# mLSTM gate logits from unsplit fp32 operands in four column groups of TensorE, with their weights loaded and folded later

## The chip, the cores and the metric

The kernel runs on one core of one Trainium2 chip. The metric is the device time of one execution in microseconds; three runs of the kernel before gave 780.39, 780.52 and 783.86, so the median is 780.52.

## The reference, cut to what matters

One encoder block on x of 512 positions by 1024 channels, batch 1, all in float32. After an RMSNorm, one projection of 10,240 columns feeds two branches: a Fourier branch (four groups of 256 channels) and an mLSTM branch (four heads of 512 channels). What the change touches is the mLSTM's gates:

```python
x_c = silu(centred_dwconv(x_m, conv_w, conv_b))      # 512 x 2048
q = block_diag_proj(x_c, w_q); k = block_diag_proj(x_c, w_k); v = block_diag_proj(x_m, w_v)   # blocks of 4
qkv = concatenate([q, k, v], axis=-1)
i_fwd = qkv @ w_igate_fwd + b_igate_fwd              # 4 heads; likewise f_fwd, i_bwd, f_bwd: 16 rows in all
```

The gate rows then go through a log-sigmoid, a cumulative sum and a running maximum, from which the heads' decay weights are made.

## The kernel before, in words

**Numbers.** A product of two fp32 matrices is made on TensorE from split operands: each tile is written once as its rounded high part (ScalarE, `hi_of`, L85) and once as the rest (VectorE, `lo_of`, L88), both in the one-pass type fp32r, and `mm3` (L93 to L97) adds high*high, high*low and low*high in PSUM. A few products (L310, L423, L618, L650 and the Fourier ones) take plain fp32 tiles instead; the trace shows each of these, the transposes of L650 apart, as two records with a weight load each.

**Weights and units.** Weights come as units of 128x1024 through `raw` (three buffers), issued on SP's queue by `fetch`; `prepare` splits them into `whi`/`wlo` (two buffers), `unit` hands the next one out. A projection unit (`proj`) is 8 x 3 = 24 products of 512 columns into one of four PSUM banks `acc`.

**The projection stage.** Seventeen units: one z unit (n = 0), then sixteen x units (n = 1 to 16) in the order `XO`. `norm_rows` (hooked in at unit 2, product group 2) makes the sums of squares, their scaling on VectorE and a power on GpSimd (L301 to L303); `norm_bcast` (hooked in by `RB_AT` at the start of unit 3) spreads the result over the partitions with four ScalarE copies, one fp32 product (L310) and a copy into `rb`. From there on `evac` (L356) takes units out of `acc`. `conv` then makes one x tile's centred convolution (one ScalarE and four VectorE instructions) and SiLU, and splits both the x tile (`vhi`, `vlo`, `so`, ...) and the convolved tile (`phi`, `plo`, ...) for the gate products.

**The gates.** `load_gates` (after unit `LOAD_AT`) brings six 256 KB pieces of gate weights over SP's queue. `fold_gates` (at `FOLD_AT`) multiplies each piece with the block-diagonal weights on GpSimd (L273), sums over four on VectorE (L274), and splits the two folded matrices into the high and low columns of `w_gate[0]` and `w_gate[1]` (L279, L280), 16 + 16 columns each. `gate_mm` (L291) then makes four products of 512 columns per tile into one bank of 32 rows: 16 tiles, 64 products. The bank is read in `gate_chain`, where a selection product (L423) adds the parts.

**Sums for later.** The last stages use sums of weight blocks that are made DRAM to DRAM. `sum_job` (called in `unit` from unit index `JOB_AT`, every third) issues a 1 MB copy on SP's queue (L156) and an accumulating one on GpSimd's (L160).

**Order.** The program order is not the order on the engines. A planner in the compiler orders each engine's instructions by their estimated ready times, earlier ones in the program first. `pin` holds an instruction behind the one traced just before it on the same engine, and nothing more. So an instruction with no inputs to wait for can move far ahead, and one that is pinned behind it can too: the load of `gb` (L414) is issued at 13.7 us though `gate_chain` comes much later in the program.

Of the kernel before, what the change touches and what calls it, by code (L numbers as in the profile page):

```python
# [8 lines left out]
F32 = mybir.dt.float32  # L9
F32R = mybir.dt.float32r  # L10
# [4 lines left out]
S = 512  # L15
D = 1024
P = 128
# [1 line left out]
EPS = 1e-6  # L19
NRAW = 3  # L20
NG = 16
JOB_AT, JOB_STEP = 8, 3
NWARM = 13
XO = (4, 5, 6, 7, 8, 9, 10, 11, 12, 13, 14, 15, 0, 1, 2, 3)
NU0 = 3
SSQ_AT, RB_AT = (2, 2), (3, 0)
LOAD_AT, FOLD_AT, CONV_AT, DRAIN_AT = 1, 4, 5, 12
Z_FIRST = 3
LOW = ("ones", "mhalf", "warm", "vecs", "raw", "whi", "wlo", "consts", "rb", "rc", "rr", "ss", "fss", "gb")
HIGH = ("sz0", "sz1", "so0", "so1", "t2k")  # L30
# [8 lines left out]
def hybrid_block(ctx: ExitStack, tc, xT, xn, units, blocks, vecs, gates, gbias, consts, dft, fnw, out):  # L39
# [37 lines left out]
    def bank(tag, cols=512, rows=P):  # L77
        count[0] += 1
        return ps.tile([rows, cols], F32, tag=tag, name=f"{tag}_{count[0]}", bufs=4)
# [4 lines left out]
    def hi_of(dst, src, scale=1.0):  # L84
        se.activation(dst, src, AF.Copy, scale=scale)  # L85
# [4 lines left out]
    def pin(ins, on=True):  # L90
        return tc.keep_in_program_order(ins) if on else ins
# [153 lines left out]
            ve.tensor_tensor(out=part[0], in0=part[0], in1=part[k], op=ALU.add)  # L245
        sqs.append(part[0])

    w_gate = [tl(f"wf{j}", [P, 16, 32], F32R) for j in range(2)]
    m4 = tl("m4", [P, 16, 4])
    prod = tl("em_r", [P, 16, 4, 4])  # L250
    ve.tensor_tensor(out=prod, in0=wkr, in1=wview(V_WQ).unsqueeze(2).to_broadcast([P, 16, 4, 4]), op=ALU.mult)
# [12 lines left out]
    def fold_gates():  # L264
        folded.append(True)
        folds = [tl("sa0", [P, 2, 16, 16]), tl("sb0", [P, 1, 16, 16])]
        for j, off in enumerate((V_WQ, V_WK, V_WV)):
            dst = folds[j // 2][:, j % 2]
            for half in range(2):
                hs = slice(8 * half, 8 * half + 8)  # L270
                g = grep[j, half]
                w = wview(off)[:, hs].unsqueeze(2).to_broadcast([P, 8, 16, 4])
                pin(gp.tensor_tensor(out=g, in0=g, in1=w, op=ALU.mult))  # L273
                ve.tensor_reduce(out=dst[:, hs, :], in_=g, axis=AX.X, op=ALU.add)  # L274
        f = folds[0]
        ve.tensor_tensor(out=f[:, 0], in0=f[:, 0], in1=f[:, 1], op=ALU.add)
        for j in range(2):
            src = folds[j][:, 0]
            se.activation(w_gate[j][:, :, 0:16], src, AF.Copy)  # L279
            ve.tensor_tensor(out=w_gate[j][:, :, 16:32], in0=src, in1=w_gate[j][:, :, 0:16].bitcast(F32), op=ALU.subtract)  # L280

    gate_ps = bank("wk", rows=32)
    pending = []
    xm, xc = {}, {}

    def gate_mm(item, last):
        p, i, ops = item
        n = 0
        for j, (h, l) in enumerate(ops):
            for r in (h, l):  # L290
                te.matmul(gate_ps, w_gate[j][:, i, :], r, start=p == 0 and n == 0, stop=last and n == 3)  # L291
                n += 1

    rb = tl("rb", [P, S])
    rc = tl("rc", [P, 4])
# [14 lines left out]
        te.matmul(rbp, ones, diag.rearrange("p b c -> p (b c)"), start=True, stop=True)  # L310
        se.activation(rb, rbp, AF.Copy)

    slots = ["plo", "so", "phi", "vhi", "vlo"]
    kept = []

    def conv(i):
        p = len(xc)
        while pending and pending[0][0] <= (p - 5 if p < 12 else p - 4):
            if not folded:
                fold_gates()  # L320
            gate_mm(pending.pop(0), False)
        src = xm[i]
        cv = t2k()
        cw = [col(V_CW + 5 * i + k) for k in range(5)]
        se.activation(cv, src, AF.Identity, scale=cw[2], bias=col(V_CB + i))
        for k, o, s in ((0, slice(2, 512), slice(0, 510)), (1, slice(1, 512), slice(0, 511)),
                        (3, slice(0, 511), slice(1, 512)), (4, slice(0, 510), slice(2, 512))):
            ve.scalar_tensor_tensor(out=cv[:, o], in0=src[:, s], scalar=cw[k], in1=cv[:, o], op0=ALU.mult, op1=ALU.add)  # L328
        if p >= 12:
            xmh, xml, xch, xcl = (tl(f"{t}{i}", [P, S], F32R) for t in ("vhi", "vlo", "phi", "plo"))  # L330
            kept.append((xch, xcl))
        elif p % 5 == 1:
            pr = [tl(f"so{n}", [P, 2, S], F32R) for n in range(2)]
            xmh, xml, xch, xcl = pr[0][:, 0, :], pr[0][:, 1, :], pr[1][:, 0, :], pr[1][:, 1, :]
        else:
            xmh, xml, xch, xcl = (tl(f"{slots[p % 5]}{n}", [P, S], F32R) for n in range(4))
        hi_of(xmh, src)
        lo_of(xml, src, xmh)
        xc[i] = tl(f"sb{i}", [P, S])
        se.activation(xc[i], cv, AF.Silu)  # L340
        hi_of(xch, xc[i])
        lo_of(xcl, xc[i], xch)
        pending.append((p, i, ((xch, xcl), (xmh, xml))))

    def proj(hooks={}):
        wh, wl = unit()
# [25 lines left out]
    for n, (kind, i) in enumerate([("z", 0)] + [("x", i) for i in XO]):  # L372
        hooks = {}
        for (at, k), fn in ((SSQ_AT, norm_rows), (RB_AT, norm_bcast)):
            if at == n:
                hooks[k] = fn
        acc = proj(hooks)
        if kind == "z":
            new_sz()
            waiting.append((None, sz[i], acc, AF.Silu))  # L380
        else:
            xm[i] = tl(f"sa{i}", [P, S])
            waiting.append((i, xm[i], acc, None))
        if n >= RB_AT[0]:
            for j, *args in waiting:
                evac(*args)
                if j is not None:
                    ready.append(j)
            waiting.clear()
        if n == LOAD_AT:  # L390
            load_gates()
        if n == FOLD_AT and not folded:
            fold_gates()
        if n >= CONV_AT and ready:
            conv(ready.pop(0))
        while n >= DRAIN_AT and ready:
            conv(ready.pop(0))
        while folded and len(pending) > (1 if n < DRAIN_AT else 2):
            gate_mm(pending.pop(0), False)
    for d in range(1, Z_FIRST):  # L400
        z_unit(d)
    while pending:
        item = pending.pop(0)
        gate_mm(item, not pending)

    a_col = tl("a_col", [P, 4, 64])
    em_r = tl("em_r", [P, S], F32R)
# [3 lines left out]
    def gate_chain():  # L411

        gb = tl("gb", [64, 2])
        nc.sync.dma_start(gb, gbias)  # L414
        graw = t2k()
        se.activation(graw[0:32, :], gate_ps, AF.Copy)
        spare = [tl(t, [64, 2, S]) for t in ("so0", "so1")]
        s0, s1, s2, s3 = spare[0][:, 0, :], spare[0][:, 1, :], spare[1][:, 0, :], spare[1][:, 1, :]
        s4, s5 = tl("wf2", [64, S]), tl("wf3", [64, S])
        ig, z, e, u, w = s0, s1, s2, s3, s4  # L420
        for j, t in enumerate((ig, z)):
            sp = bank("acc", rows=64)
            te.matmul(sp, ident_c[0:32, C_SEL + 64 * j : C_SEL + 64 * j + 64], graw[0:32, :], start=True, stop=True)  # L423
            se.activation(t[0:32, :], sp[0:32, :], AF.Identity, bias=gb[0:32, j : j + 1])
            se.activation(t[32:64, ::-1], sp[32:64, :], AF.Identity, bias=gb[32:64, j : j + 1])
        se.activation(e, z, AF.Abs)
        se.activation(e, e, AF.Exp, scale=-1.0)
        ve.tensor_scalar(out=u, in0=e, scalar1=1.0, scalar2=None, op0=ALU.add)
        ve.scalar_tensor_tensor(out=w, in0=u, scalar=-1.0, in1=e, op0=ALU.add, op1=ALU.subtract)
        se.activation(u, u, AF.Ln)  # L430
        ve.scalar_tensor_tensor(out=w, in0=z, scalar=0.0, in1=w, op0=ALU.min, op1=ALU.add)
        ve.tensor_tensor(out=w, in0=w, in1=u, op=ALU.subtract)
        fc = e
        ve.tensor_tensor_scan(out=fc, data0=ones[0:64, 0:1].to_broadcast([64, S]), data1=w, initial=0.0,
                              op0=ALU.mult, op1=ALU.add)
# [12 lines left out]
        return an  # L448
# [527 lines left out]
def _layouts(inputs):  # L976
# [63 lines left out]
    for dr in range(2):  # L1040
        for h in range(4):
            consts[32 * dr + h, C_BSEL + 4 * dr + h] = 1.0
            consts[64 + 32 * dr + h, C_BSEL + 4 * dr + h] = 1.0
            for j in range(2):
                for part in range(2):
                    consts[16 * part + 8 * j + 4 * dr + h, C_SEL + 64 * j + 32 * dr + h] = 1.0
    sc = 1.0 / np.sqrt(512.0 * 256.0)
    c = np.arange(256)[:, None]
    k = np.arange(129)[None, :]
# [30 lines left out]
```

## Time and profile before

| | |
|---|---|
| Median of three runs | 780.52 us (780.39 to 783.86) |
| The profiled execution | 782.93 us, its span 781.0 us |
| TensorE (PE) busy | 766.3 us, 98% of the span |
| VectorE (DVE), ScalarE (ACT), GpSimd (POOL) busy | 525.0, 417.4, 67.2 us |
| Mean granted TensorE clock | 0.995 of full speed |

Times in rows are microseconds from the span's start unless a column says ns. A matmul's record lasts longer than the place it takes, since the next one starts while it drains; what a product costs in a gapless stretch is the distance between starts. "busy" of an instruction that is held up by another engine includes the hold. In the waits and in brackets after a row, the name behind `<-` is what ended the idle time.

### The profile page before, as it was taken

Reading aid. Unit: us, or ns where it says so; the run is one execution under the profiler, and the core shown is the slowest. Engines: PE = TensorE matmul, PEld = TensorE weight load, DVE = VectorE, ACT = ScalarE, POOL = GpSimd, SP = SyncE. Lnnn points to the kernel's source line nnn. Section 1 sums busy time; section 2 is a strip of 40 time slices with the busy share of each in tenths; the row PEclk is TensorE's granted clock in tenths of the full one; section 3 lists DMA queues with packets and bytes.
Section 4 is the critical chain, followed back from the end, with each engine's and each line's share of the span. In section 5 each row is a group of like instructions: output and inputs, shape, how many; then the busy total and the mean of one; then the engine's idle time right before and its main releaser. Section 6 shows DMA issues by size and latency. Waiting matters only on the chain.

```text
span 781.0 us, 10974 instructions
## 1 busy us (share of the span) xinstructions
PE 766.3 (98%) x4182; PEld 654.9 (84%) x4182; DVE 525.0 (67%) x802; ACT 417.4 (53%) x658; POOL 67.2 (9%) x139
## 2 busy tenths in 40 slices
PE   9799999999999999999999999999999999999996
PEld 7587777778888888888888888899999999988885
DVE  6799998577857664777485972156676787446632
ACT  7356556568646743685363542266544587534422
POOL 0400000010210210021101000000011100000021
PEclk9999999999999999999999999999999999999999
DMA  8747762054363545155604582366555356445511
GB/s 300 235 141 209 214 179 92 28 161 138 80 189 102 167 109 162 42 174 154 197 27 162 141 257 90 105 193 217 190 161 159 121 166 192 144 144 169 172 55 55
DMA packets 39446, 117.03 MB, mean 150 GB/s; under 512 B 4577, under 2 KB 5090, under 8 KB 35298
## 3 DMA queue, kind: packets, MB, share of 16 engines
q1 hardware_dynamic: 37090, 99.56, 37.8%
q0 software_dynamic: 2304, 16.78, 11.2%
q8 instruction: 33, 0.54, 0.3%
q14 instruction: 19, 0.16, 0.1%
HBM read 114.22 MB, written 35.65 MB: 192 GB/s over the span
## 4 chain that ended last, share of the span: by engine, by line
PE 93%; DVE 2%; DMA 2%; ACT 2%; issue 0%; SPq 0%; POOL 0%; POOLq 0%; ACTq 0%; DVEq 0%
PE acc L95 16%; PE acc L97 16%; PE acc L96 16%; PE wk L95 7%; PE wk L97 7%; PE wk L96 7%; PE acc L548 3%; PE acc L547 3%; PE acc L549 3%; PE wk L291 2%; PE acc L955 2%; PE acc L953 2%; PE acc L954 2%; PE wk L618 2%; DMA raw<-in_units_dram 2%; DVE wlo L88 1%
## 5 line engine op out<-in xcount | busy, mean ns | idle before, releaser
L88 DVE TENSOR_TENSOR wlo<-raw,whi 128x1024 fp32r<-128x1024 f32 (+1 forms) x103 | 128.4, 1249 | 84.0 <-ACT whi L85 83.9
L85 ACT ACTIVATE whi<-raw 128x1024 fp32r<-128x1024 f32 (+1 forms) x103 | 106.4, 1034 | 135.2 <-PE acc L96 98.0
L97 PE MATMUL acc<-hhi,wlo 128*128 128x512 f32 x248 | 97.3, 393 | 4.3 <-DVE wlo L88 4.3
L95 PE MATMUL acc<-hhi,whi 128*128 128x512 f32 x248 | 97.8, 397 | 0.8 <-ACT whi L85 0.8
L96 PE MATMUL acc<-hlo,whi 128*128 128x512 f32 x248 | 97.7, 394 | 0.0
L97 PEld LDWEIGHTS acc<-hhi,wlo 128*128 128x128 f32 x248 | 47.0, 190 | 15.5 <-DVE wlo L88 4.7
L95 PEld LDWEIGHTS acc<-hhi,whi 128*128 128x128 f32 x248 | 46.8, 189 | 11.6 <-ACT whi L85 1.2
L96 PEld LDWEIGHTS acc<-hlo,whi 128*128 128x128 f32 x248 | 47.0, 190 | 11.3 <-DVE hlo L199 0.7
L549 PE MATMUL acc<-whi,hlo 128*128 128x512 f32 x128 | 50.4, 394 | 0.0
L548 PE MATMUL acc<-wlo,hhi 128*128 128x512 f32 x128 | 50.4, 393 | 0.0
L96 PE MATMUL acc<-sb,whi 128*128 128x512 f32 x128 | 49.9, 391 | 0.0
L95 PE MATMUL acc<-sa,whi 128*128 128x512 f32 x128 | 49.8, 390 | 0.1
L96 PE MATMUL wk<-vlo,phi 128*128 128x512 f32 x128 | 49.8, 389 | 0.0
L95 PE MATMUL wk<-vhi,phi 128*128 128x512 f32 x128 | 49.8, 390 | 0.0
L97 PE MATMUL acc<-sa,wlo 128*128 128x512 f32 x128 | 48.6, 391 | 0.0
L97 PE MATMUL wk<-vhi,plo 128*128 128x512 f32 x128 | 48.0, 389 | 0.0
L547 PE MATMUL acc<-whi,hhi 128*128 128x512 f32 x128 | 47.7, 393 | 0.0
L328 DVE SCALAR_TENSOR_TENSOR t2k<-sa,vecs,t2k 128x511 f32<-128x511 f32 (+1 forms) x64 | 45.6, 739 | 0.0
L88 DVE TENSOR_TENSOR gwl<-raw,gwh 128x1024 fp32r<-128x1024 f32 x27 | 33.0, 1222 | 15.9 <-ACT gwh L85 15.9
L85 ACT ACTIVATE gwh<-raw 128x1024 fp32r<-128x1024 f32 x27 | 28.6, 1059 | 18.3 <-PE acc L96 8.3
L95 PEld LDWEIGHTS wk<-vhi,phi 128*128 128x128 f32 x128 | 24.0, 188 | 5.8 <-issue 0.8
L95 PEld LDWEIGHTS acc<-sa,whi 128*128 128x128 f32 x128 | 24.0, 188 | 5.4 <-ACT whi L85 0.5
(352 smaller groups left out, 1956.9 us busy)
## 6 DMA issues: line engine op xcount, KB each, us to landing
raw<-in_units_dram SPq DMA_DIRECT2D x77, 512.0 KB, 3.4
sum<-in_blocks_dram SPq DMA_DIRECT2D x16, 1024.0 KB, 6.5
raw<-sum SPq DMA_DIRECT2D x64, 256.0 KB, 3.8
raw<-in_blocks_dram SPq DMA_DIRECT2D x48, 256.0 KB, 3.7
sum<-in_blocks_dram POOLq DMA_DIRECT2D x8, 1024.0 KB, 8.2
sum<-sum POOLq DMA_DIRECT2D x8, 1024.0 KB, 8.8
xr<-in_xT_dram SPq DMA_DIRECT2D x8, 256.0 KB, 4.2
yb<-in_xn_dram SPq DMA_DIRECT2D x8, 256.0 KB, 2.6
```

Source lines behind the costliest of these rows:

```text
L85: se.activation(dst, src, AF.Copy, scale=scale)
L88: ve.tensor_tensor(out=dst, in0=src, in1=hi.bitcast(F32), op=ALU.subtract)
L95: pin(te.matmul(acc, wh, xh, start=start, stop=False, **skip), pinned)
L96: te.matmul(acc, wh, xl, start=False, stop=False, **skip)
L97: te.matmul(acc, wl, xh, start=False, stop=stop, **skip)
L291: te.matmul(gate_ps, w_gate[j][:, i, :], r, start=p == 0 and n == 0, stop=last and n == 3)
L328: ve.scalar_tensor_tensor(out=cv[:, o], in0=src[:, s], scalar=cw[k], in1=cv[:, o], op0=ALU.mult, op1=ALU.add)
L547: te.matmul(ops[t], hv(x_hi, k)[:, ts], wh[:, ks], start=k == 0, stop=False)
L548: te.matmul(ops[t], hv(x_hi, k)[:, ts], wl[:, ks], start=False, stop=False)
L549: te.matmul(ops[t], hv(x_lo, k)[:, ts], wh[:, ks], start=False, stop=k == 7)
L618: te.matmul(vp[:, ds], xm[c0 + d][:, b * P : (b + 1) * P], vbf[:, d, :], start=True, stop=True)
L953: te.matmul(acc, m_hi[k][:, ts], wh, start=k == 0, stop=False)
```

## The change

- The x tiles and convolved tiles are no longer split for the gates; only the last four convolved tiles still are (they are used by the first head).
- `gate_mm` takes the fp32 tiles themselves. It runs on four tiles (two pairs) at a time, once more than four are pending. Each of the eight products has 32 weight columns (16 used, 16 zero) and goes to one of four groups of 32 columns of the array, and so to one of four groups of 32 rows of a 128-row bank: convolved and x tile, of the first and of the second of a pair. 32 fp32 products replace 64 of type fp32r.
- `w_gate` is plain fp32, zeroed at the start on GpSimd; the split of the folded weights goes.
- The six multiplications of the fold move from GpSimd to VectorE.
- Gate weights are loaded after unit 6 instead of 1, and folded at unit 10 instead of 4; `conv` begins at unit 4 instead of 5.
- `norm_bcast` is hooked in at product group 6 of unit 2 instead of at the start of unit 3.
- `JOB_AT` goes from 8 to 11.
- The selection product adds four row groups instead of two.

```diff
-JOB_AT, JOB_STEP = 8, 3
+JOB_AT, JOB_STEP = 11, 3
-SSQ_AT, RB_AT = (2, 2), (3, 0)
-LOAD_AT, FOLD_AT, CONV_AT, DRAIN_AT = 1, 4, 5, 12
+SSQ_AT, RB_AT = (2, 2), (2, 6)
+LOAD_AT, FOLD_AT, CONV_AT, DRAIN_AT = 6, 10, 4, 12
...
-    w_gate = [tl(f"wf{j}", [P, 16, 32], F32R) for j in range(2)]
+    w_gate = [tl(f"wf{j}", [P, 16, 32]) for j in range(2)]
+    for j in range(2):
+        gp.memset(w_gate[j], 0.0)
...
-                pin(gp.tensor_tensor(out=g, in0=g, in1=w, op=ALU.mult))
+                ve.tensor_tensor(out=g, in0=g, in1=w, op=ALU.mult)
                 ve.tensor_reduce(out=dst[:, hs, :], in_=g, axis=AX.X, op=ALU.add)
         f = folds[0]
-        ve.tensor_tensor(out=f[:, 0], in0=f[:, 0], in1=f[:, 1], op=ALU.add)
-        for j in range(2):
-            src = folds[j][:, 0]
-            se.activation(w_gate[j][:, :, 0:16], src, AF.Copy)
-            ve.tensor_tensor(out=w_gate[j][:, :, 16:32], in0=src, in1=w_gate[j][:, :, 0:16].bitcast(F32), op=ALU.subtract)
-
-    gate_ps = bank("wk", rows=32)
+        ve.tensor_tensor(out=w_gate[0][:, :, 0:16], in0=f[:, 0], in1=f[:, 1], op=ALU.add)
+        se.activation(w_gate[1][:, :, 0:16], folds[1][:, 0], AF.Copy)
+    gate_ps = bank("wk")
...
-    def gate_mm(item, last):
-        p, i, ops = item
-        n = 0
-        for j, (h, l) in enumerate(ops):
-            for r in (h, l):
-                te.matmul(gate_ps, w_gate[j][:, i, :], r, start=p == 0 and n == 0, stop=last and n == 3)
-                n += 1
+    def gate_mm(items):
+        for a in range(0, len(items), 2):
+            for b in range(2):
+                p, i = items[a + b]
+                for j, r in enumerate((xc[i], xm[i])):
+                    rows = slice(32 * (2 * b + j), 32 * (2 * b + j) + 32)
+                    te.matmul(gate_ps[rows, :], w_gate[j][:, i, :], r, start=p < 2, stop=p >= 14,
+                              tile_position=(0, 32 * (2 * b + j)))
...
-        if p >= 12:
-            xmh, xml, xch, xcl = (tl(f"{t}{i}", [P, S], F32R) for t in ("vhi", "vlo", "phi", "plo"))
-            kept.append((xch, xcl))
-        elif p % 5 == 1:
...
-        hi_of(xmh, src)
-        lo_of(xml, src, xmh)
         xc[i] = tl(f"sb{i}", [P, S])
         se.activation(xc[i], cv, AF.Silu)
-        hi_of(xch, xc[i])
-        lo_of(xcl, xc[i], xch)
-        pending.append((p, i, ((xch, xcl), (xmh, xml))))
+        if p >= 12:
+            xch, xcl = (tl(f"{t}{i}", [P, S], F32R) for t in ("phi", "plo"))
+            hi_of(xch, xc[i])
+            lo_of(xcl, xc[i], xch)
+            kept.append((xch, xcl))
+        pending.append((p, i))
...
-        while folded and len(pending) > (1 if n < DRAIN_AT else 2):
-            gate_mm(pending.pop(0), False)
+        if folded and len(pending) >= 5:
+            gate_mm([pending.pop(0) for _ in range(4)])
     for d in range(1, Z_FIRST):
         z_unit(d)
-    while pending:
-        item = pending.pop(0)
-        gate_mm(item, not pending)
+    gate_mm(pending)
```

## Rows read from the trace of the kernel before

**Rows 1.** The page's busy time of each engine, and the busy time by stretch (us of the stretch, then PE, PEld, DVE, ACT, POOL busy with instruction counts, granted clock, DMA share, GB/s).

```profile
PE 766.3 (98%) x4182; PEld 654.9 (84%) x4182; DVE 525.0 (67%) x802; ACT 417.4 (53%) x658; POOL 67.2 (9%) x139
...
0.00:33.00 33.00, 26.12 (x119) 20.97 (x120) 21.48 (x26) 18.40 (x33) 8.96 (x17) 1.00 0.88 285
33.00:140.00 107.00, 107.00 (x462) 82.62 (x462) 100.55 (x147) 63.80 (x95) 4.21 (x5) 0.98 0.57 167
...
30.00:40.00 10.00, 7.24 (x25) 5.83 (x26) 10.00 (x13) 3.64 (x6) 1.61 (x2) 0.83 0.44 130
```

**Rows 2.** What PE waited for in the first 200 us (us in total, times, longest).

```profile
PE acc L97 <- DVE wlo L88: 4.3, 1, 4.3
PE wk L181 <- POOL half L457: 1.1, 1, 1.1
PE acc L95 <- ACT whi L85: 0.8, 1, 0.8
PE wk L310 <- ACT sa L308: 0.7, 1, 0.7
```

**Rows 3.** The timeline of VectorE, GpSimd, ScalarE and SP's queue around 24 us (start, duration, engine, line, what).

```profile
13.71 0.55 SPq L414 DMA_DIRECT2D gb<-in_gbias_dram  x1
14.94 0.54 SPq L156 DMA_DIRECT2D sum<-in_blocks_dram  x1
15.57 1.01 SPq L126 DMA_DIRECT2D raw<-in_units_dram  x2
...
22.01 0.16 DVE L302 TENSOR_SCALAR rc<-wk 128x4 f32<-128x4 f32 x1 [2.05 <-PE wk L301]
23.25 1.08 POOL L160 DMA_DIRECT2D sum<-in_blocks_dram  x1 [21.99 <-DMA sum<-in_blocks_dram]
24.17 1.36 POOL L303 TENSOR_TENSOR rc<-rc,mhalf 128x4 f32<-128x4 f32 x1
24.27 1.06 ACT L85 ACTIVATE whi<-raw 128x1024 fp32r<-128x1024 f32 x1 [6.25 <-DMA raw<-in_units_dram]
25.20 3.39 POOL L273 TENSOR_TENSOR sa<-sa,vecs 128x512 f32<-128x512 f32 x3
25.36 7.35 DVE L88 TENSOR_TENSOR wlo<-raw,whi 128x1024 fp32r<-128x1024 f32 x1 [3.19 <-ACT whi L85]
25.56 1.28 ACT L308 ACTIVATE sa<-consts,rc 128x128 f32<-128x128 f32 x4 [0.23 <-POOL rc L303]
28.26 3.35 POOL L273 TENSOR_TENSOR sb<-sb,vecs 128x512 f32<-128x512 f32 x3
33.82 1.21 DVE L88 TENSOR_TENSOR wlo<-raw,whi 128x1024 fp32r<-128x1024 f32 x1
```

**Rows 4.** PE's timeline from the last sums of squares (L301) to the return of the full clock; from 21.84 to 25.78 it has 18 products without a gap.

```profile
21.61 0.36 PE L301 MATMUL wk<-ones,sb 128*128 128x1 f32 x2
21.84 0.48 PE L95 MATMUL acc<-hhi,so 128*128 128x512 f32 x1
...
25.78 0.39 PE L97 MATMUL acc<-hhi,so 128*128 128x512 f32 x1
26.89 1.13 PE L310 MATMUL wk<-sa,ones 128*128 128x512 f32 x2 [0.72 <-ACT sa L308]
...
28.09 0.39 PE L96 MATMUL acc<-hlo,whi 128*128 128x512 f32 x1
32.76 0.58 PE L97 MATMUL acc<-hhi,wlo 128*128 128x512 f32 x1 [4.29 <-DVE wlo L88]
33.13 0.63 PE L95 MATMUL acc<-hhi,whi 128*128 128x512 f32 x1
...
36.51 0.39 PE L97 MATMUL acc<-hhi,wlo 128*128 128x512 f32 x1
36.74 0.40 PE L95 MATMUL acc<-hhi,whi 128*128 128x512 f32 x1
```

**Rows 5.** The gate products: one of the groups by tile (durations min/median/max in ns, weights 128*32), and two pieces of the chain of waits (start, length, what).

```profile
L291 PE MATMUL wk<-plo,wf x16: 387/392/398, 56.3 to 137.8; 128*32 128x512 f32 x16
...
81.58 0.93 PE wk L291 x4
...
98.71 0.93 PE wk L291 x4
```

**Rows 6.** The plain fp32 products in the chain of waits: L423 (32 rows, 64 weight columns, 512 moving columns) and L618 (128x128, 128 moving columns), each record one of two per product; and L618's form by line (busy us, mean ns).

```profile
140.91 1.86 PE acc L423 x4
...
170.87 1.56 PE wk L618 x14
...
178.85 1.78 PE wk L618 x16
...
L618 PE MATMUL wk<-mhi,sa 128*128 128x128 f32 x128 | 16.7, 274 | 0.0
```

**Rows 7.** The timeline around L423 (PE products and PEld weight loads).

```profile
140.53 0.39 PE L95 MATMUL wk<-vhi,phi 128*128 128x512 f32 x1
140.84 0.19 PEld L423 LDWEIGHTS acc<-t2k,consts 32*64 32x64 f32 x2 [0.35 <-issue]
140.85 1.93 PE L423 MATMUL acc<-t2k,consts 32*64 32x512 f32 x4
...
142.70 0.19 PEld L95 LDWEIGHTS wk<-vhi,phi 128*128 128x128 f32 x1 [0.81 <-issue]
142.70 0.50 PE L95 MATMUL wk<-vhi,phi 128*128 128x512 f32 x1
...
143.04 0.39 PE L96 MATMUL wk<-vlo,phi 128*128 128x512 f32 x1
```

**Rows 8.** VectorE and ScalarE instructions by form between 33 and 140 us (busy us, mean ns, idle before): the weight split, one of the gate splits on each engine, the fold's sums, and a VectorE product with a broadcast operand.

```profile
L88 DVE TENSOR_TENSOR wlo<-raw,whi 128x1024 fp32r<-128x1024 f32 x17 | 20.7, 1215 | 0.7 <-ACT whi L85 0.7
L88 DVE TENSOR_TENSOR plo<-sb,phi 128x512 fp32r<-128x512 f32 x4 | 2.7, 680 | 0.0
L274 DVE TENSOR_REDUCE sa<-sa 128x128 f32<-128x512 f32 x3 | 1.9, 672 | 0.0
L471 DVE TENSOR_TENSOR t2k<-m,consts 128x512 f32<-128x512 f32 x1 | 0.7, 682 | 0.0
...
L85 ACT ACTIVATE phi<-sb 128x512 fp32r<-128x512 f32 x6 | 3.8, 628 | 0.1
```

More of the change, by code (lines that the diff above doesn't have):

```diff
@@ L311, in norm_bcast @@
         se.activation(rb, rbp, AF.Copy)
-    slots = ["plo", "so", "phi", "vhi", "vlo"]
     kept = []
@@ L317, in conv @@
         p = len(xc)
-        while pending and pending[0][0] <= (p - 5 if p < 12 else p - 4):
-            if not folded:
-                fold_gates()
-            gate_mm(pending.pop(0), False)
         src = xm[i]
@@ L328, in conv @@
             ve.scalar_tensor_tensor(out=cv[:, o], in0=src[:, s], scalar=cw[k], in1=cv[:, o], op0=ALU.mult, op1=ALU.add)
-        if p >= 12:
-            xmh, xml, xch, xcl = (tl(f"{t}{i}", [P, S], F32R) for t in ("vhi", "vlo", "phi", "plo"))
-            kept.append((xch, xcl))
-        elif p % 5 == 1:
[L333 to L336, printed above, removed]
-        hi_of(xmh, src)
-        lo_of(xml, src, xmh)
         xc[i] = tl(f"sb{i}", [P, S])
         se.activation(xc[i], cv, AF.Silu)
-        hi_of(xch, xc[i])
-        lo_of(xcl, xc[i], xch)
-        pending.append((p, i, ((xch, xcl), (xmh, xml))))
+        if p >= 12:
[4 more added lines that the diff above has]
+        pending.append((p, i))
     def proj(hooks={}):
@@ L397, in hybrid_block @@
             conv(ready.pop(0))
-        while folded and len(pending) > (1 if n < DRAIN_AT else 2):
-            gate_mm(pending.pop(0), False)
+        if folded and len(pending) >= 5:
+            gate_mm([pending.pop(0) for _ in range(4)])
     for d in range(1, Z_FIRST):
         z_unit(d)
-    while pending:
-        item = pending.pop(0)
-        gate_mm(item, not pending)
+    gate_mm(pending)
     a_col = tl("a_col", [P, 4, 64])
@@ L415, in gate_chain @@
         graw = t2k()
-        se.activation(graw[0:32, :], gate_ps, AF.Copy)
+        se.activation(graw, gate_ps, AF.Copy)
         spare = [tl(t, [64, 2, S]) for t in ("so0", "so1")]
@@ L422, in gate_chain @@
             sp = bank("acc", rows=64)
-            te.matmul(sp, ident_c[0:32, C_SEL + 64 * j : C_SEL + 64 * j + 64], graw[0:32, :], start=True, stop=True)
+            te.matmul(sp, ident_c[:, C_SEL + 64 * j : C_SEL + 64 * j + 64], graw, start=True, stop=True)
             se.activation(t[0:32, :], sp[0:32, :], AF.Identity, bias=gb[0:32, j : j + 1])
@@ L1044, in _layouts @@
             for j in range(2):
-                for part in range(2):
-                    consts[16 * part + 8 * j + 4 * dr + h, C_SEL + 64 * j + 32 * dr + h] = 1.0
+                for part in range(4):
+                    consts[32 * part + 8 * j + 4 * dr + h, C_SEL + 64 * j + 32 * dr + h] = 1.0
     sc = 1.0 / np.sqrt(512.0 * 256.0)
```

## The prediction, made before the changed kernel ran

> **What bounds the kernel now.** I read the busy time first, whole and by stretch. TensorE works for 766 of 781 us, and from 33 to 140 us, where the gates are made, it never pauses: 107.0 of 107.0 us [rows 1]. VectorE is next, busy for 100.6 of those 107 us. So in that stretch only what changes TensorE's own work changes the time; VectorE's load counts only if it grows. The first 33 us are different: PE works for 26.1 us of them, and the list of its waits has one large entry, 4.3 us for one weight split [rows 2]. The timelines show its cause: the split starts at 25.36 and takes 7.35 us, where the next of its kind takes 1.21 [rows 3]. It ends when GpSimd's six multiplications of the fold (25.20 to 31.6) are over: for that time VectorE got nothing done that PE needed. Then the clock: the ten microseconds from 30 have a mean granted clock of 0.83 [rows 1], and after the pause the products start 0.43 us apart instead of 0.227 until 36.5 [rows 4], the lower of the two levels, 1.2 instead of 2.4 GHz.
>
> **The start of the kernel.** Three terms, in starts of PE instructions [rows 4].
>
> (a) The pause goes, since no multiplication is left on GpSimd. The product at 28.09 should have been followed at 28.32; the next one started at 32.76: 4.4 us. What is late next in its place? Unit 3's weights landed at 24.27 behind 1.5 MB of gate weights and a 1 MB block copy; the gate weights now come after unit 6, so unit 3 comes no later. Its two splits take 1.06 and 1.21 us [rows 3], and PE reaches unit 3 at about 27 us: no wait follows.
>
> (b) Without the pause the clock stays up. From 32.76 to 36.51 nine products took 3.75 us instead of 9 x 0.227 = 2.04: 1.7 us. The other two runs of the kernel before are some 2.5 us shorter than the profiled one, so they may have lost less here; I take 1.7, with 0 as the low end.
>
> (c) `norm_bcast` moves from the end of unit 2 to 12 products after the sums of squares, 21.84 + 12 x 0.227 = 24.6. Its chain is the scaling (ends 22.17), GpSimd's power (1.36), four copies (1.28) and hand-overs. Before, the power stood behind a block-sum DMA on GpSimd until 24.17 [rows 3]. That one is a job traced after the `gb` load: the copy at 14.94 is pinned to it and so floats to the front. With `JOB_AT` 11 a job falls on the same place in the program (20 - 8 and 20 - 11 are both multiples of 3), so a 1 MB copy still floats; but it is then job 3, and the accumulating DMA after it needs results of jobs 1 and 2, so it can't stand ahead of the power. The chain then ends at about 22.2 + 0.1 + 1.36 + 1.28 + 0.1 = 25.0, and PE waits 0.4 us for it. Before, the product started at 26.89 where 26.0 was possible, 0.9 us. Gain 0.5; from 0 (GpSimd held as before) to 0.9.
>
> Together 4.4 + 1.7 + 0.5 = 6.6 us, between 4.4 and 7.0.
>
> **The gate products.** Before: four in 0.93 us, so 64 x 0.2325 = 14.9 us of gapless PE time [rows 5]. After: 32 fp32 products, which are 64 records, each of two passes. A record of 512 columns isn't there in a full-speed stretch; its price is bounded by L423, 1.86 / 4 = 0.465, and by L618, 1.56 / 14 = 0.111 for 128 columns, four times that 0.446 [rows 6]. I take 0.445; narrow weights (L423) load late, which groups of eight would hide. One after another, that is 28.5 us. What the column groups give back no row shows: every product of this kernel writes from row 0 and has the whole array to itself. Neighbouring products of the change use different groups, but the two records of one product use the same one. If records start in the order of issue, the second record of a product waits for the first and holds up all behind it; then it runs beside the first record of the next product. A run of n products takes n + 1 record times. With four runs of eight: 36 x 0.445 = 16.0 us. To this comes the change of mode: around L423 the products start 0.32 and 0.34 us apart where 0.227 is usual, 0.1 us at each end [rows 7], 0.2 per run, 0.8 for four. So 16.8 us, 1.9 more than before. The ends: all four groups at once, 16 x 0.445 + 0.8 = 7.9 (7.0 less than before); none, 28.5 + 0.8 = 29.3 (14.4 more). I take the middle since it is what issue in order gives; if the planner puts other products between, each further run costs 0.445 + 0.2.
>
> The Trainium skill's page "TensorE: Matmul & The Clock Gate" (Part 3: Packing small matmuls) has matmuls of different tiles overlap while they start and end strictly in the order of issue, which is the middle case. Its page "TensorEngine Tiling (Array Packing)" (Key Properties) says that a change of tiling mode drains the engine; the 0.1 us at each end of L423 would be that.
>
> **What lies beside other work.** 28 gate splits go on each of two engines: 28 x 0.68 = 19.0 us on VectorE, 28 x 0.63 = 17.6 on ScalarE [rows 8]. PE never waited for either from 33 to 140 us, so this gives nothing. The six multiplications add 6 x 0.68 = 4.1 us to VectorE, which has 16 us net more room by then; I cost them at nothing (rival D has the case without room). The zeroing of `w_gate` is two writes on GpSimd, idle from 1.3 to 23 us. The six gate loads now stand on SP's queue behind unit 9's weights, with unit 10's behind them. SP's issues take up to about half a microsecond, so these come some 3 us later, while two units of 5.4 us each are split or ready ahead: nothing; at most the 3 us. The block sums are first used after unit 63 and the last job moves by one step, to unit index 59; on GpSimd every later job stands where one stood before: nothing. An earlier `conv` fills VectorE while it idles.
>
> **Sum.** The profiled execution took 782.9 us for a span of 781.0. 782.9 - 6.6 + 1.9 = 778.2; against the median, which is 2.4 lower, 780.5 - 6.6 + 1.9 = 775.8: 776.
>
> **The rivals.**
>
> A, slower: the column groups don't overlap; the gate block is 14.4 us longer, and 780.5 - 6.6 + 14.4 = 788.3. The kernel becomes slower once 64 records take more than 14.9 + 6.6 - 0.8 = 20.7 us, 47 record times. For it: no row shows two products in the array at once, and both records of L423, with a quarter of the array's rows, had it to themselves. Against it: the groups share no cell and no output row.
>
> C: four records run side by side, because a record that waits for its group doesn't hold up the others: 780.5 - 6.6 - 7.0 = 766.9. For it: neighbours are four different groups. Against it: it needs a record to overtake the one ahead, and in the timeline every product starts in the order of its weight load. "TensorEngine Tiling (Array Packing)" in the Trainium skill (Key Properties) says that tiles operate independently, with weight loads and matmuls in parallel; taken at its word that is C, and no row here decides.
>
> D: the fold on VectorE becomes PE's wait. Six multiplications, six sums and an addition, close to 0.6 us apart, are 7.5 us. A weight split may start when the unit two before it is done, so it has 5.4 + 0.5 - 1.1 - 1.2 = 3.6 us to spare; a fold in one piece ahead of it stops PE for 3.9: 775.8 + 3.9 = 779.7. For it: VectorE is 94% busy there today. Against: the planner puts ready instructions in gaps, as it did with the sums of the fold, and the load falls by 16 us.
>
> E, the change doesn't do what it says: something else holds the split of unit 3, and the pause stays. Then 780.5 + 1.9 = 782.4. Against it: the pause's only cause in the rows is on GpSimd.
>
> **How the numbers follow.** Forecast 0.38, C 0.29, A 0.17, D 0.11, E 0.05. Half a per cent, 3.9 us, is about what a measurement of this kernel can tell from no change: faster is below 776.6, slower above 784.4. Faster: all of C, 0.23 of the forecast's 0.38 (it lies 0.8 from that bound and one run more costs 0.65), 0.01 of D: 0.53. Same: 0.15 of the forecast, 0.10 of D, 0.05 of E: 0.30. Slower: A, 0.17. The range from 764.5 to 783.5 takes in all but A. The likeliest case alone reaches from 775 (terms b and c at their best) to 779 (b at half, three runs more).
>
> **What would show it.** (a) No entry of PE waiting for `wlo` in the first 40 us, and no split near 7 us. (b) Granted clock 1.00 from 30 to 40 us. (c) L310 starts near 25.0. Gates: records of 32 weight columns start in pairs, a pair every 0.445 us; single ones every 0.445 us show A, four to 0.445 us show C. D: a wait of PE for `wlo` near 70 us with L273's successors just before it on VectorE. The prediction is wrong if the gate records together hold PE for much less or more than 17 us, or if a new wait stands in the first 33 us.

## The result, and the profile after

Fifteen runs of the changed kernel have a median of 776.04 us (775.46 to 776.96), fifteen of the kernel before 780.52 (775.57 to 783.86): a ratio of 0.9947, 95% interval 0.9927 to 0.9967. The forecast was 776.0. The profiled execution took 776.38 us.

The page's span and busy times of the changed kernel answer to [rows 1]:

```profile
span 774.7 us, 10917 instructions
...
PE 763.4 (99%) x4182; PEld 647.3 (84%) x4182; DVE 507.0 (65%) x778; ACT 401.0 (52%) x629; POOL 61.7 (8%) x135
```

Its busy time in the same three stretches as in [rows 1], with the same columns:

```profile
0.00:33.00 33.00, 30.99 (x142) 24.89 (x143) 17.45 (x29) 19.96 (x35) 2.54 (x12) 1.00 0.70 237
33.00:140.00 107.00, 105.61 (x462) 75.05 (x461) 87.05 (x120) 50.87 (x71) 4.61 (x5) 1.00 0.56 163
30.00:40.00 10.00, 10.00 (x43) 7.71 (x42) 8.29 (x13) 5.43 (x7) 0.00 (x0) 1.00 0.17 53
```

PE is busy 4.9 us longer in the first 33 us, and at full clock from 30 to 40 us. From 33 to 140 us it had no pause before; now 1.39 us are missing. The list of what PE waited for from 9 to 200 us says where:

```profile
PE acc L95 <- ACT whi L85: 1.4, 2, 0.9
PE wk L577 <- ACT vhi L85: 0.5, 1, 0.5
```

The entry of 4.3 us for `wlo` [rows 2] is gone, and a pair for `whi` is new. (Line numbers have moved: the broadcast L310 is now L311, `evac` L345, the fold L275 and L276, the gate products L292.)

A ledger over the projection stage needs marks. I take the starts of the 96th and the 480th projection product (L95 to L97), the last of the fourth and of the twentieth unit of 24. The timeline of the kernel before has them here:

```profile
39.27 0.39 PE L97 MATMUL acc<-hhi,wlo 128*128 128x512 f32 x1
...
157.35 0.39 PE L97 MATMUL acc<-hhi,wlo 128*128 128x512 f32 x1
```

The changed kernel's timeline around the start:

```profile
22.78 1.02 POOL L304 TENSOR_TENSOR rc<-rc,mhalf 128x4 f32<-128x4 f32 x1 [20.60 <-DVE rc L303]
...
29.94 1.02 PE L311 MATMUL wk<-sa,ones 128*128 128x512 f32 x2
...
31.71 0.69 DVE L345 TENSOR_TENSOR sz<-acc,rb 128x512 f32<-128x512 f32 x1 [7.50 <-ACT rb L312]
...
32.19 0.39 PE L97 MATMUL acc<-hhi,wlo 128*128 128x512 f32 x1
...
151.05 0.39 PE L97 MATMUL acc<-hhi,wlo 128*128 128x512 f32 x1
```

So the start gains 39.27 - 32.19 = 7.1 us, and the later mark, like the span, 6.3. The gates add 1.4 to the 7.1, and 2.2 go back.

**The gates.** Their timeline, the longest run of records and a short one:

```profile
67.46 0.39 PE L97 MATMUL acc<-hhi,wlo 128*128 128x512 f32 x1
67.78 0.62 PE L292 MATMUL wk<-sb,wf 128*32 128x512 f32 x1
67.78 0.62 PE L292 MATMUL wk<-sa,wf 128*32 128x512 f32 x1
67.79 0.62 PE L292 MATMUL wk<-sb,wf 128*32 128x512 f32 x1
67.80 0.62 PE L292 MATMUL wk<-sa,wf 128*32 128x512 f32 x1
68.23 0.59 PE L292 MATMUL wk<-sb,wf 128*32 128x512 f32 x1
...
69.63 0.50 PE L97 MATMUL acc<-hhi,wlo 128*128 128x512 f32 x1
69.97 0.40 PE L95 MATMUL acc<-hhi,whi 128*128 128x512 f32 x1
...
121.15 1.04 PE L292 MATMUL wk<-sb,wf 128*32 128x512 f32 x2
122.13 0.50 PE L95 MATMUL acc<-hhi,whi 128*128 128x512 f32 x1
```

Four records start within 0.02 us, and the next four 0.43 us later: all four groups work side by side. As the cost of a run I take the time from the last product ahead of it to the second behind it, less 2 x 0.227. The long run of 16 records (eight products) costs 69.97 - 67.46 - 0.45 = 2.06; runs of 4 to 6 records cost 1.2, and so does the single product at 121.15. The planner made ten runs, 13.6 us in all; the kernel before spent 15.0 by the same measure, in 26 runs.

**What goes back.** From 32.19 the next 144 products, all ahead of the first gate run, take 34.81 us; at the 5.44 us that a unit of 24 takes in a gapless stretch they would take 32.64. That is the 2.2 us. Most of it stands at the two new waits. The changed kernel's timeline at the first of them:

```profile
53.45 1.22 DVE L88 TENSOR_TENSOR wlo<-raw,whi 128x1024 fp32r<-128x1024 f32 x1
54.32 1.06 ACT L85 ACTIVATE whi<-raw 128x1024 fp32r<-128x1024 f32 x1 [1.07 <-PE acc L96]
54.35 0.39 PE L95 MATMUL acc<-hhi,whi 128*128 128x512 f32 x1
54.58 0.39 PE L96 MATMUL acc<-hlo,whi 128*128 128x512 f32 x1
55.44 0.50 PE L95 MATMUL acc<-hhi,whi 128*128 128x512 f32 x1 [0.47 <-ACT whi L85]
55.77 0.40 PE L96 MATMUL acc<-hlo,whi 128*128 128x512 f32 x1
56.01 0.40 PE L97 MATMUL acc<-hhi,wlo 128*128 128x512 f32 x1
```

The usual order is L95, L96, L97. Here L95 and L96 come twice before the L97. The program's order on TensorE, with the tiles numbered, tells why (`acc_112` is the next unit):

```
L95 MATMUL acc_105_548<-hhi0_14_122,whi_95_501 128x512 [waits Activation_49]
L96 MATMUL acc_105_548<-hlo0_18_126,whi_95_501 128x512
L95 MATMUL acc_112_589<-hhi0_14_122,whi_102_542 128x512 [waits Activation_49]
L96 MATMUL acc_112_589<-hlo0_18_126,whi_102_542 128x512
L97 MATMUL acc_105_548<-hhi0_14_122,wlo_96_502 128x512 [waits DVE_49]
```

The planner put two products of the next unit ahead of the product that needs the low part. But the next unit's split has to wait for one of the two `whi` buffers, until the unit before is done (54.32), and PE stands until it is finished. The low part that the planner was avoiding was ready at 53.45 + 1.22 = 54.67, before the 54.81 at which its product could have started. The same order stands one unit on (a wait of 0.92 us until 62.11). With the slow restarts (54.58 to 55.44 and 60.80 to 62.11 where 0.23 is usual, then 0.1 each) the two cost 1.9 of the 2.2 us.

The medians differ by 4.5, not 6.3 to 6.5: the profiled run of the kernel before lies 2.4 above its median.

### The profile page after: what moved, and what is told of

Its sections match the earlier page's. It is cut to its first block, busy times and chain, and to the rows that moved or that the text cites. A ratio compares the mean times of both kernels' runs of the same rounds, so it can differ in the third digit from the quotient of the medians.

```text
span 774.7 us, 10917 instructions
## 1 busy us (share of the span) xinstructions
PE 763.4 (99%) x4182; PEld 647.3 (84%) x4182; DVE 507.0 (65%) x778; ACT 401.0 (52%) x629; POOL 61.7 (8%) x135
## 4 chain that ended last, share of the span: by engine, by line
PE 96%; ACT 1%; DVE 1%; DMA 1%; SPq 0%; issue 0%; POOL 0%; POOLq 0%; ACTq 0%
PE acc L95 17%; PE acc L97 17%; PE acc L96 17%; PE wk L97 7%; PE wk L95 7%; PE wk L96 7%; PE acc L534 3%; PE acc L535 3%; PE acc L536 3%; PE acc L942 2%; PE acc L941 2%; PE acc L940 2%; PE wk L605 2%; PE wk L292 1%; PE wk L637 1%; DMA raw<-in_units_dram 1%
## 5 line engine op out<-in xcount | busy, mean ns | idle before, releaser
L88 DVE TENSOR_TENSOR wlo<-raw,whi 128x1024 fp32r<-128x1024 f32 (+1 forms) x103 | 122.3, 1190 | 80.6 <-ACT whi L85 80.3
L95 PE MATMUL acc<-hhi,whi 128*128 128x512 f32 x248 | 97.2, 395 | 1.7 <-ACT whi L85 1.7
L97 PE MATMUL acc<-hhi,wlo 128*128 128x512 f32 x248 | 97.2, 393 | 0.0
L96 PE MATMUL acc<-hlo,whi 128*128 128x512 f32 x248 | 97.0, 391 | 0.0
L95 PEld LDWEIGHTS acc<-hhi,whi 128*128 128x128 f32 x248 | 46.5, 188 | 15.0 <-ACT whi L85 4.6
L97 PEld LDWEIGHTS acc<-hhi,wlo 128*128 128x128 f32 x248 | 46.6, 188 | 14.7 <-DVE sa L345 2.5
L96 PEld LDWEIGHTS acc<-hlo,whi 128*128 128x128 f32 x248 | 46.6, 188 | 10.0 <-DVE hlo L199 0.7
L96 PE MATMUL acc<-sb,whi 128*128 128x512 f32 x128 | 49.9, 391 | 0.0
L95 PE MATMUL acc<-sa,whi 128*128 128x512 f32 x128 | 49.8, 390 | 0.1
L96 PE MATMUL wk<-vlo,phi 128*128 128x512 f32 x128 | 49.8, 389 | 0.0
L95 PE MATMUL wk<-vhi,phi 128*128 128x512 f32 x128 | 49.6, 390 | 0.0
L97 PE MATMUL acc<-sa,wlo 128*128 128x512 f32 x128 | 48.6, 391 | 0.0
L97 PE MATMUL wk<-vhi,plo 128*128 128x512 f32 x128 | 48.0, 389 | 0.0
L95 PEld LDWEIGHTS wk<-vhi,phi 128*128 128x128 f32 x128 | 24.0, 188 | 5.7 <-PE acc L410 0.8
L95 PEld LDWEIGHTS acc<-sa,whi 128*128 128x128 f32 x128 | 24.0, 188 | 5.4 <-ACT whi L85 0.5
```

The lines of the kernel that those rows point to most:

```text
L88: ve.tensor_tensor(out=dst, in0=src, in1=hi.bitcast(F32), op=ALU.subtract)
L95: pin(te.matmul(acc, wh, xh, start=start, stop=False, **skip), pinned)
L96: te.matmul(acc, wh, xl, start=False, stop=False, **skip)
L97: te.matmul(acc, wl, xh, start=False, stop=stop, **skip)
```

## The experiments

Twelve runs. A median stands with its ratio to the kernel before, timed on the same chip; one profiled execution each gives the marks. The changed kernel was timed with the result alone, so a difference from it sets two medians of different timings side by side; its own fifteen runs lie within 1.5 us.

**1. The kernel before, with only the fold's multiplications on VectorE.**

```diff
-                pin(gp.tensor_tensor(out=g, in0=g, in1=w, op=ALU.mult))
+                ve.tensor_tensor(out=g, in0=g, in1=w, op=ALU.mult)
```

> The kernel before with one edit: the six multiplications of the fold on VectorE instead of GpSimd. Theory 1 (the 7.35 us weight split and PE's 4.3 us pause come from GpSimd's multiplications): no weight split over 1.5 us after 20 us, no wait of PE for it in the first 40 us, full clock from 30 to 40 us; about 4.4 + 1.7 us less, 774 to 777. Rival (unit 3 is late because its transfer is late): the pause stays, 779 to 782.

Median 779.78, ratio 0.9992 (0.9964 to 1.0019): the cause of the pause was right, the time a miss. The 4.3 us pause is gone, but the unpinned multiplications now stand on VectorE ahead of work that PE needs. Timeline:

```profile
20.12 1.28 DVE L273 TENSOR_TENSOR sa<-sa,vecs 128x512 f32<-128x512 f32 x2
20.25 0.50 PE L96 MATMUL acc<-hlo,whi 128*128 128x512 f32 x1 [0.52 <-DVE hlo L199]
...
22.05 0.38 PE L301 MATMUL wk<-ones,sb 128*128 128x1 f32 x2 [0.60 <-DVE sb L245]
```

and the stretches behind it:

```profile
20.00:25.00 5.00, 4.15 (x20) 3.53 (x21) 3.22 (x7) 2.12 (x2) 1.07 (x1) 0.80 1.03 372
25.00:30.00 5.00, 5.00 (x14) 3.90 (x13) 4.42 (x7) 1.28 (x4) 1.96 (x1) 0.52 1.02 236
```

After the two short pauses the clock is at its lower level until 29.8, with 14 products in 5 us where 22 fit. The 96th product starts at 37.16: only 2.1 us gained. Taking the multiplications off GpSimd is not enough.

**2. The changed kernel, with the multiplications back on GpSimd** (the line of run 1, the other way).

> The changed kernel with one edit undone: the six multiplications back on GpSimd, pinned as before. Theory 1: wherever they run, a VectorE instruction with two operands in SBUF is held up for some 6.7 us in all; VectorE is full there and a weight split has about 3.6 us to spare, so PE waits some 3 us: 778 to 780. Rival (only the place at 25 us made it costly): 775 to 777, or less, since VectorE is relieved of 4.1 us.

778.68, ratio 0.9996 (0.9966 to 1.0027): 2.6 slower than the changed kernel, as expected. Timeline:

```profile
46.94 4.32 POOL L275 TENSOR_TENSOR sa<-sa,vecs 128x512 f32<-128x512 f32 x3 [23.51 <-ACT sb L326]
51.22 4.53 POOL L275 TENSOR_TENSOR sb<-sb,vecs 128x512 f32<-128x512 f32 x3
...
63.09 0.79 PE L97 MATMUL acc<-hhi,wlo 128*128 128x512 f32 x1 [2.48 <-DVE wlo L88]
```

The start keeps its gain (96th product at 32.21), so the late place alone clears it, wherever the multiplications run. A pause for `wlo` comes back behind the fold's new place, with a granted clock of 0.78 from 60 to 65 us, in place of the pair for `whi`; the gates cost 14.4.

**3. All gate products in one column group** (a bank of 32 rows, same sums).

```diff
-    gate_ps = bank("wk")
+    gate_ps = bank("wk", rows=32)
...
-                    te.matmul(gate_ps[rows, :], w_gate[j][:, i, :], r, start=p < 2, stop=p >= 14,
-                              tile_position=(0, 32 * (2 * b + j)))
+                    te.matmul(gate_ps, w_gate[j][:, i, :], r, start=p + j == 0, stop=p + j == 16,
+                              tile_position=(0, 0))
```

> The changed kernel with all 32 gate products in one column group and one group of 32 rows of the bank; the same sums, made one after another. Theory 2 (the column groups let products run at once): 64 records at 0.43 us are 27.5 us plus about 0.34 us for each run of them, so 14 to 18 us more than the changed kernel, 790 to 794. Rival (narrow fp32 products overlap anyway, or PE's time isn't set by them): 776 to 779.

792.83, ratio 1.017 (1.012 to 1.022), 16.8 above the changed kernel; the gates take 30.1 us. Timeline:

```profile
67.65 1.04 PE L291 MATMUL wk<-sb,wf 128*32 128x512 f32 x2
68.54 1.02 PE L291 MATMUL wk<-sa,wf 128*32 128x512 f32 x2
69.39 1.02 PE L291 MATMUL wk<-sb,wf 128*32 128x512 f32 x2
```

Products 0.857 us apart, two records of 0.428 each: what rival A would have been.

**4. Gates at the end of the program, unpinned.**

```diff
-        if folded and len(pending) >= 5:
-            gate_mm([pending.pop(0) for _ in range(4)])
```

> The changed kernel with all 32 gate products in one go after the last projection unit. Theory 2: a run costs two records' time (0.86 us) for every four products begun plus 0.34 us, so one run of 32 products takes 7.2 us instead of the 13.6 us of the ten runs in the changed kernel: 6.4 us less, about 770. Rival (the gate chain then starts later and the first head waits for it): most of that comes back as a wait of PE between 140 and 175 us, 773 to 778.

775.35, ratio 0.9927 (0.99 to 0.9953): a miss. The planner floated the products forward again, in nine runs, 12.4 us.

**5. The same, each gate product pinned.**

```diff
-                    te.matmul(gate_ps[rows, :], w_gate[j][:, i, :], r, start=p < 2, stop=p >= 14,
-                              tile_position=(0, 32 * (2 * b + j)))
+                    pin(te.matmul(gate_ps[rows, :], w_gate[j][:, i, :], r, start=p < 2, stop=p >= 14,
+                                  tile_position=(0, 32 * (2 * b + j))))
```

> The changed kernel with all 32 gate products after the last projection unit and each pinned behind the one before, so that they stay one run. Theory 2 (four products at a time, 0.34 us for each run of them): 16 record times of 0.428 us plus 0.34 us is 7.2 us, where the ten runs of the changed kernel take 13.6; 6.4 us less, 769 to 771. Rival (the runs stood where PE would have waited for weight splits or the gate chain, so packing them uncovers those waits): new waits of PE between 60 and 175 us, 773 to 777.

769.54, ratio 0.988 (0.9826 to 0.9934). One run of 64 records; the chain of waits has it as

```profile
115.76 7.00 PE wk L292 x64
```

7.2 us with its ends, 6.4 less than in ten runs; the time fell by 6.5. The price of a run follows: 64 records in fours are 16 starts, 16 x 0.428 (run 3) = 6.85, and 0.35 remains for the run itself.

**6. As 5, with the two products of each column group next to each other in the order of issue.**

```diff
-        for a in range(0, len(items), 2):
-            for b in range(2):
-                p, i = items[a + b]
-                for j, r in enumerate((xc[i], xm[i])):
+        for a in range(0, len(items), 4):
+            for b in range(2):
+                for j in range(2):
+                    for c in range(2):
+                        p, i = items[a + 2 * c + b]
+                        r = (xc, xm)[j][i]
```

> As a_end_pinned, but in each block of eight products the two of one column group stand next to each other. Theory 3 (products start in the order of issue, and one whose group is busy holds up those behind it): each pair of neighbours of one group costs two record times, 34 in all, 14.6 us plus 0.34, about 7.7 us more than a_end_pinned. Rival (a product of a free group overtakes): 7 to 8 us for the run, as in a_end_pinned.

770.48 in a single run; the gates take 7.28 us. Instructions are issued sb, sb, sa, sa; the timeline shows

```profile
116.57 0.62 PE L294 MATMUL wk<-sb,wf 128*32 128x512 f32 x1
116.58 0.62 PE L294 MATMUL wk<-sa,wf 128*32 128x512 f32 x1
116.59 0.62 PE L294 MATMUL wk<-sb,wf 128*32 128x512 f32 x1
116.61 0.62 PE L294 MATMUL wk<-sa,wf 128*32 128x512 f32 x1
```

A start of every group within 0.04 us: a product whose group is free does not wait behind one whose group is busy. Starts strictly in order fall.

**7. The changed kernel, with the gate weights loaded and folded early.**

```diff
-LOAD_AT, FOLD_AT, CONV_AT, DRAIN_AT = 6, 10, 4, 12
+LOAD_AT, FOLD_AT, CONV_AT, DRAIN_AT = 1, 4, 4, 12
```

> The changed kernel with the gate weights loaded after unit 1 and folded at unit 4 as before, the multiplications still on VectorE. Theory 4 (it takes the late load as well: early multiplications stand ahead of the last splits of x on VectorE, PE pauses shortly and its clock falls): pauses of about 0.5 us near 20 us, a granted clock well below 1 between 20 and 30 us, 3 to 4 us more than the changed kernel, 779 to 780. Rival (moving the multiplications was enough): 775 to 777.

781.34, ratio 1.003 (0.9998 to 1.0062): the whole gain is gone. The pauses of run 1 are back (0.52 at 20.07, 0.61 at 21.88), but in the profiled execution, 779.69, the clock stayed up:

```profile
20.00:25.00 5.00, 4.32 (x25) 3.54 (x26) 3.51 (x8) 1.65 (x2) 0.00 (x0) 1.00 1.01 344
25.00:30.00 5.00, 5.00 (x24) 4.12 (x23) 5.00 (x9) 1.75 (x5) 1.93 (x1) 1.00 0.66 219
```

So there the start costs only 1.6 us (96th product at 33.79), and the rest has another reason than the one given: the gates, ready earlier, come in 14 runs instead of 10, 17.4 us, 3.8 more. The pair of waits for `whi` is absent, 2.2 less; together 3.2 of the 3.3 us between the two profiled executions. The other 2 us of the median are not in this profile: the three executions above 782.7 us have a mean granted clock of 0.993, the two below 780 have 0.997 and 0.999.

**8. The changed kernel, with the hook of `norm_bcast` and `JOB_AT` as before.**

```diff
-JOB_AT, JOB_STEP = 11, 3
+JOB_AT, JOB_STEP = 8, 3
-SSQ_AT, RB_AT = (2, 2), (2, 6)
+SSQ_AT, RB_AT = (2, 2), (3, 0)
```

> The changed kernel with two edits undone: the norm's broadcast at the start of unit 3 and the block sums from unit index 8. As the prediction has it: the accumulating DMA stands ahead of the power on GpSimd again, and the broadcast is 1 to 2 us later; PE loses about 0.5 us, 776 to 777. Rival (these two edits carry a large part of the 7.1 us gained by unit 4): 778 to 780, with a wait of PE before 40 us.

773.75, ratio 0.9921 (0.9892 to 0.995): 2.3 better than the changed kernel, a miss of mine. Timeline:

```profile
19.37 1.07 POOL L160 DMA_DIRECT2D sum<-in_blocks_dram  x1 [17.19 <-DMA sum<-in_blocks_dram]
...
26.23 1.02 PE L311 MATMUL wk<-sa,ones 128*128 128x512 f32 x2
...
27.92 0.69 DVE L345 TENSOR_TENSOR sz<-acc,rb 128x512 f32<-128x512 f32 x1 [3.82 <-ACT rb L312]
```

With the earlier hook the broadcast runs later: 29.94 against 26.23. VectorE then stood idle for 7.5 us where it is 3.8 here. With the old hook the pair of waits for `whi` is gone, the program's order on TensorE has no product of the next unit ahead of an L97, and the gates come in eight runs, 12.9 us.

**9 and 10. As 5, with the old hook; and with the old `JOB_AT` too** (lines of run 8).

> a_end_pinned with the norm's broadcast at the start of unit 3 again, the block sums still from index 11. Theory 5 (the hook in unit 2 made the planner put the broadcast behind unit 3, so that VectorE idled 7.5 us and PE waited 1.4 us later): broadcast near 26 us, no waits of PE at 55 and 62 us, 1.4 to 2.3 us less than a_end_pinned, 767 to 768. Rival (the gain of a_rb_job_old came from the block sums): 769 to 770.

> As a_end_pinned_rb_old, and the block sums from index 8 again. Theory 5: the block sums' place changes nothing, so the same as a_end_pinned_rb_old within 0.5 us, 767 to 768. Rival (they matter): 1 us or more apart from it.

768.08 (767.51 to 769.05), ratio 0.9849 (0.9793 to 0.9906), and 768.22, ratio 0.985 (0.9793 to 0.9906). Both beat both kernels; the place of the block sums changes nothing. The page of run 9:

```profile
span 766.5 us, 10911 instructions
...
PE 757.4 (99%) x4182; PEld 649.3 (85%) x4182; DVE 505.7 (66%) x778; ACT 402.5 (53%) x629; POOL 62.1 (8%) x135
```

No wait for `whi` is left in the projection stage, and the gates cost 7.2 us.

**11. The kernel before, with the multiplications on VectorE and the late places, its gates split as they were.**

```diff
-LOAD_AT, FOLD_AT, CONV_AT, DRAIN_AT = 1, 4, 5, 12
+LOAD_AT, FOLD_AT, CONV_AT, DRAIN_AT = 6, 10, 5, 12
-                pin(gp.tensor_tensor(out=g, in0=g, in1=w, op=ALU.mult))
+                ve.tensor_tensor(out=g, in0=g, in1=w, op=ALU.mult)
```

> The kernel before with the multiplications on VectorE, the gate weights loaded after unit 6 and folded at unit 10; the gate products as before, from split operands. Theory 4 (multiplications on VectorE and late loads together make the whole gain at the start): no pause, full clock to 40 us, unit 4's products end 6 to 7 us earlier than before, gate products 15 us: 775 to 777. Rival (with all 32 splits VectorE has no room for the fold): a wait of PE for a weight split of 2 to 4 us between 45 and 90 us, 778 to 780.

781.97, ratio 1.0014 (0.998 to 1.0049). The start has its gain, 6.4 us (96th product at 32.91), and loses it again. What PE waited for from 30 to 200 us:

```profile
PE acc L506 <- DVE mx_r L446: 1.6, 1, 1.6
PE acc L95 <- ACT whi L85: 1.4, 2, 0.9
PE wk L291 <- DVE plo L88: 0.6, 1, 0.6
PE acc L547 <- DVE sz L356: 0.6, 1, 0.6
```

Three of the four entries are VectorE coming late. The fourth is the pair for `whi` again (55.98 and 62.66 us), with the old hook this time. The gates cost 16.5, waits among them included. A miss, beyond the rival too: with the 28 gate splits still on VectorE, the early start was worth nothing here.

**12. The kernel before once more.**

> The kernel before once more, unchanged. Its runs spread from 775.2 to 784.7, those of the changed kernel over 1.5 us. Theory 6 (the pause hangs on which of GpSimd's first multiplication, at 25.20 us, and VectorE's split, at 25.36 us, starts first): with the order of the first profile, a split of about 7 us and 780 to 783; with the other order, a split near 1.2 us, no pause, and about 776. Rival (the spread has another source): a run near 776 with the pause, or near 782 without.

779.59 in a single run. The same cause, a smaller pause; GpSimd's first multiplication (23.39) starts ahead of the split here too, so the other order was not seen:

```profile
23.73 6.10 DVE L88 TENSOR_TENSOR wlo<-raw,whi 128x1024 fp32r<-128x1024 f32 x1 [1.46 <-ACT whi L85]
29.88 0.50 PE L97 MATMUL acc<-hhi,wlo 128*128 128x512 f32 x1 [2.28 <-DVE wlo L88]
```

Unit 3's weights were there at 22.6 instead of 24.3, so the held split ended 2.9 us sooner. The kernel before ran between 775.2 and 785.3 us in all, the changed one between 775.5 and 777.0; a pause whose length hangs on an arrival fits that, but no run near 775 has a profile, so what happens in those stays open. Their clock is on record: of the 57 executions of the kernel before that were timed beside these runs, the 15 under 777 us have a mean granted clock of 0.997 to 0.999, the changed kernel's own, and the 35 above 781 have 0.993 to 0.996. So the change takes away the long executions; the shortest ones of the kernel before were already as short.

## Why the prediction was right, and where it was not

The time was right by errors that cancel. The forecast's sum was -6.6 + 1.9 = -4.7 us. Between the profiled executions it is -7.1 for the start, -1.4 for the gates (3.3 better than forecast) and +2.2 for new waits and restarts, which the sum did not have: -6.3. Between the medians it is -4.5, since the profiled execution of before lay 2.4 above its median and that of after 0.3. The prediction took the whole gain off the median, though it saw that other runs were shorter and priced that only as the low end of (b). (It speaks of "the other two runs"; there were three, and the third, 783.86, was 0.9 longer than the profiled one.)

**The start, (a) and (b): the size right, the reason in part.** No wait for `wlo` in the first 40 us, no split longer than 1.23 us, granted clock 1.00 from 30 to 40. In all 7.1 us against 6.6. But (a) credits the engine alone ("since no multiplication is left on GpSimd"). Run 1, with the multiplications early on VectorE, loses the pause and yet gains only 2.1, since they hold up VectorE's own work that PE needs; run 2 has the whole gain at the start with them on GpSimd, so the late place is enough. What the move to VectorE gives is that the late fold makes no pause for `wlo` (2.48 us in run 2).

**(c): the gain at the top of its range, its way wrong.** "The chain then ends at about 25.0" failed. The power was free early (22.78), as predicted, but the planner put the broadcast behind products of unit 3, at 29.94. PE no longer waits for it, so (c) gained its full 0.9 where the sum had 0.5. That is the 7.1: 4.4 + 1.7 + 0.9 = 7.0. The price came later, by way of VectorE's idling (below). Run 8 shows that the old hook has the same gain without the price: with the gate weights late, the accumulating DMA that held up the power starts at 19.37 instead of 23.25 [rows 3].

**The gates: the step that failed is "the second record of a product waits for the first and holds up all behind it".** Four records run side by side, which is rival C by the prediction's own sign; run 6 shows the overtaking that it needs. The price of a record was right (0.428 against 0.445). "With four runs of eight" failed too, to the other side: the planner made ten. Four runs of 16 records would have cost 4 x 2.05 = 8.2; ten cost 13.6; forecast were 16.8. The two errors had opposite signs. C's price for four runs, 7.9, was close to the 8.2; the ten runs and the new waits kept the changed kernel from C's 766.9, and run 9, with one run and without those waits, comes within 1.2 of it.

The Trainium skill's page "TensorE: Matmul & The Clock Gate" (Part 3: Packing small matmuls) has matmuls start and end strictly in the order of issue. The forecast took that side, and run 6 differs: 7.28 us in an order that would keep groups waiting, 7.20 in the other. The measurement decides. "TensorEngine Tiling (Array Packing)" (Key Properties) has tiles as independent, which agrees, and a drain at a change of mode; the 0.35 us per run above the records agree with a cost of that kind.

**What was costed at nothing.** The fold on VectorE did become a wait of PE, in part, though not as rival D had it. D expected the fold to stand ahead of a weight split on VectorE, and PE to wait for `wlo`. On the chip `wlo` was in time; the planner's order puts it off, and that order made PE wait for `whi`. That the order causes the wait is shown by the order above together with the ready time of `wlo`. Why the planner orders so is not shown, since its estimates were not read. That it counts on a late VectorE fits: the pair stands where the fold runs late on VectorE and VectorE either idled before it (new hook: the changed kernel and runs 3 to 6) or still has the splits (run 11, old hook); it is absent with the fold on GpSimd (run 2), with the fold early (runs 1 and 7) and with the old hook without the splits (runs 8 to 10). So the hook alone does not make it.

The 28 splits were costed at nothing as well. They were hidden before, yet their removal may be the room in which the start's gain survives: run 11 keeps them and ends where it began. It differs from the changed kernel in more than the splits (the hook, `JOB_AT`, `CONV_AT`), so the share of each is not separated. The place of the block sums costs nothing, as predicted (run 10), and the list of waits from 9 to 200 us has none for a late load.

**The rivals.** A is refuted by the records and priced by run 3: 30.1 us for the gates against 29.3 in the working. E falls with the pause. D came in a small form, C as a mechanism without its time.

## What to carry to other kernels

Small-column fp32 products in four column groups cost a quarter of what they cost in one, but each run of them among full-width products costs some 0.35 us more and counts in whole fours of products; keep them in one run, pinned. When a pause of one engine goes, ask which engine the work now comes earlier to: in run 11, the one early start with VectorE's splits kept, the gain was gone by the end. After moving a hook, look at the order that came out, not at the place in the program: an earlier hook gave a later broadcast, and a wait can be made by an order that avoids another.

## What the runs showed of the hardware that was not expected

- A 512-column fp32 product with 32 weight columns is two records of 0.428 us. Four such products in four column groups take as long as one, and a product of a free group starts ahead of an earlier one whose group is busy (run 6).
- After pauses of 0.52 and 0.60 us the granted clock fell to 0.52 in the next full stretch of run 1, and after 0.52 and 0.61 us at the same place it stayed at 1.00 in run 7, with one profile each. What tells the two apart is open.
- Beside GpSimd's multiplications a VectorE weight split takes 7.35 us [rows 3] or 6.10 (run 12) instead of 1.21. The multiplications themselves go on: three in 3.39 us there [rows 3], three in 4.32 and 4.53 in run 2, where VectorE was busy almost throughout. There a split beside them (52.92) took only 1.90 us, and PE's pause was 2.48 instead of 4.3.
